# Memory attention's products in the other order, and which split the gathered rows follow

## The chip, the cores and the metric

The kernel runs on one core of one Trainium2 chip. The time is that of one launch on the device, in microseconds. Three runs of the kernel before took 4951.19, 4959.05 and 4960.37 us; their median is 4959.05 us. A further execution was profiled: it took 4954.55 us, and its trace spans 4952.8 us. All durations below are from that one trace.

The core has five instruction streams that run side by side and wait for one another by semaphores: TensorE (PE; its weight loads are shown apart, as PEld), VectorE (DVE), ScalarE (ACT), GpSimd (POOL), and SP, which here only issues transfers. POOL issues transfers too.

## The reference

One layer on 512 tokens of width 2048: a mixer (an mLSTM with 4 heads, a forgetting attention "fox" with 16 heads, two gated branches, an output product), then attention over a memory of 256 rows, then a layer of 16384 experts of which each token picks 128. Each of the three is followed by a residual and a norm. What is changed is the attention over the memory:

```python
def memory_cross_attention(x, mem, w_q, w_kv, w_o):
    q = (x @ w_q).reshape(B, S, X_HEADS, X_HD)          # 4 heads of 512
    kv = mem @ w_kv                                     # 256 x 4096
    k = kv[..., :D_MODEL].reshape(B, -1, X_HEADS, X_HD)
    v = kv[..., D_MODEL:].reshape(B, -1, X_HEADS, X_HD)
    s = jnp.einsum('bshd,bmhd->bhsm', q, k) * X_HD ** -0.5
    p = jax.nn.softmax(s, -1)
    o = jnp.einsum('bhsm,bmhd->bshd', p, v).reshape(B, S, D_MODEL)
    return o @ w_o
```

In the expert layer a token's output is the sum over its 128 experts of gelu(u.x) g v, where u and v are rows of two tables of 16384 x 2048.

## The kernel before

**Products.** A 2048-wide product runs in groups of 512 output columns. A group takes 8 loads; each load (`load_w`) brings 512 KB of weights into a buffer `raw` by a transfer from SP, ACT rounds it into a high part `whi` (L134), and DVE subtracts for the low part `wlo` (L137); with `work["share"]` at 8, POOL does every eighth subtraction instead (L136). PE then does three passes (high by high, high by low, low by high). `group_ws` holds the weights as the stationary operand: 24 matmuls for a load, as wide as there are tokens. `group_as` holds the activations: 6 matmuls of 512 columns for a load and block of 128 tokens. Plain f32 matmuls (scores, results) are not split.

**Two paths.** The first 128 tokens are path A, the other 384 path B. A has short work for a load (6 matmuls of 512), B long work (24 of 384, or 18 of 512). `weave(gen, other, rate)` takes `rate` steps of `other` for each step of `gen`, and one step at the end of a group of A. Small work between loads (scores, transposes) stands in a list `mids`, from which `ride` takes one step after each load's products. Loads go through `raw` buffers of two rings, 3 and 2 deep. Within this written order a planner that simulates the engines settles the order of each engine's instructions; SP, too, takes its transfers in order.

**Stages, with their places in the trace.** Memory keys and values (`memory`, 64 loads), woven with A's mLSTM, to 368 us. A's branch product (`branch_ml`, 64 loads), woven thinly with B's mLSTM ("heads"), to 514. A's fox (128 loads), woven likewise, to 822. A's merge, output product, norm, memory attention (`cross`, 32 loads for its queries), its output product (`residual` with `w_xo`, 32 loads), norm and expert query, woven likewise, to 1290. Then B: the rest of its mLSTM, branch, fox (1715 to 2320), merge, output product, `cross` (about 2630 to 2815), `residual` with `w_xo` (to 2963), query. Then the expert tables: from 3129 the choice of experts and products with U for the first `LOOK` = 72 of 128 blocks (`stage_a`), from 3636 the main loop, which multiplies by V and does the rest of U.

**Gathered rows.** For block A and for some tokens of B, rows of the tables come by indirect transfers that POOL issues (L846), and DVE multiplies or adds them (L874, L877, 2.3 us each). For block A these 258 steps are spread over 315 loads of path B, from B's mLSTM to its second residual. The instruction `after` ties each transfer and each use to `work["last"]`, the low-part split of the last load, whichever engine did it.

**Memory attention before.** `memory` writes keys transposed (`kmd`) and values (`vmd`) to DRAM: four groups of `group_ws` at 256 columns, four of `group_as` with two blocks. `cross` multiplies the tokens by `w_xq` head by head, then has f32 score matmuls (L719), a softmax (L723 to L726), transposes (L733) and f32 result matmuls (L741).

Of the kernel before, what the change touches and what calls it, by code (L numbers as in the profile page):

```python
# [46 lines left out]
def build(tc, I, out):  # L47
    nc = tc.nc
    with ExitStack() as ctx:
# [261 lines left out]
        vmd = dp.tile([X_H, 2, P, 512], F32, tag="vmd", name="vmd")  # L311
        mkd = dp.tile([ML_H, 2, P, P], F32, tag="mkd", name="mkd")
# [40 lines left out]
        def memory(mp):  # L353
# [8 lines left out]
            for g in range(4):  # L362
                def ev_mk(s, b, g=g, k=[]):
# [282 lines left out]
        def residual(R, pool, src, X, W, alloc, tmp, r, out):  # L646
# [3 lines left out]
            for g in range(4):  # L650
# [8 lines left out]
                yield from group_as(W[g], X, R.nb, ev)  # L659
# [39 lines left out]
        def cross(R, pool, X1, qt, kvt, pt, opair, O):  # L699
            n, nb = R.n, R.nb  # L700
            for h in range(X_H):
                q = []

                def ev_q(s, b, q=q):
                    q.append(qt())
                    nc.scalar.activation(q[s], b[:, :n], AF.Copy, scale=X_D ** -0.5)

                yield from R.group(I["w_xq"][h], X1, ev_q)
                kt2, v2 = ([kvt(), kvt()] for _ in range(2))
                for j in range(2):  # L710
                    nc.gpsimd.dma_start(kt2[j], kmd[h, j])
                    nc.gpsimd.dma_start(v2[j], vmd[h, j])
                pr, pT = [], []

                def scores(q=q, kt2=kt2, pr=pr):
                    for qb in range(nb):
                        bank = sm_bank()
                        for c in range(4):
                            nc.tensor.matmul(bank[:, :MEM], q[c][:, qb * P:(qb + 1) * P],  # L719
                                             kt2[c // 2][:, (c % 2) * MEM:(c % 2 + 1) * MEM], start=c == 0, stop=c == 3)  # L720
                        st = pool.tile([P, 4], F32, tag="xst", bufs=4, name=nm("xst"))
                        p = pool.tile([P, MEM], F32, tag="xp", bufs=nb, name=nm("xp"))
                        nc.vector.tensor_reduce(out=st[:, 0:1], in_=bank[:, :MEM], axis=AX.X, op=ALU.max, negate=True)  # L723
                        nc.scalar.activation(p, bank[:, :MEM], AF.Exp, bias=st[:, 0:1], accum_out=st[:, 1:2])
                        nc.vector.reciprocal(st[:, 2:3], st[:, 1:2])
                        nc.vector.tensor_scalar(p, p, st[:, 2:3], None, op0=ALU.mult)  # L726
                        pr.append(p)

                def turn_p(pr=pr, pT=pT):
                    for m in range(2):  # L730
                        bank = sm_bank()
                        for qb in range(nb):
                            nc.tensor.transpose(bank[:, qb * P:(qb + 1) * P], pr[qb][:, m * P:(m + 1) * P], ident)  # L733
                        pT.append(pt())
                        nc.scalar.copy(pT[m], bank[:, :n])

                def result(cs, h=h, v2=v2, pT=pT):
                    for c in cs:
                        bank = sm_bank()
                        for m in range(2):  # L740
                            nc.tensor.matmul(bank[:, :n], v2[m][:, c * P:(c + 1) * P], pT[m], start=m == 0, stop=m == 1)  # L741
                        a, b = opair(h)
# [4 lines left out]
                mid(scores, None, turn_p, lambda f=result: f((0, 1)), lambda f=result: f((2, 3)))  # L747
# [208 lines left out]
        with tc.tile_pool(name="sa", bufs=1, side="right", reuse_waits="tile") as sa:  # L956
            def aq(n=P):
                return sa.tile([P, P], F32, tag="q", bufs=11, name=nm("aq"))
# [26 lines left out]
            with tc.tile_pool(name="a1", bufs=1, side="right", reuse_waits="tile") as a1:  # L985
# [16 lines left out]
            def tail_a():  # L1002
                r, sts = [[None] * 4], []
                ra = {}
                with tc.tile_pool(name="a2", bufs=1, side="right", reuse_waits="tile") as a2:
# [9 lines left out]
                    yield from cross(A, sa, X1A, aq, at, aq, ac, OA)  # L1015
# [402 lines left out]
```

## Time and profile before

| | |
|---|---|
| median of three runs | 4959.05 us |
| profiled execution | 4954.55 us (span 4952.8 us) |
| PE busy | 4747.2 us, 96%, 28401 matmuls |
| DVE busy | 3713.1 us, 75% |
| ACT busy | 2123.3 us, 43% |
| POOL busy | 1416.2 us, 29% |
| transfers | 1420.99 MB, mean 287 GB/s |
| granted TensorE clock | 0.985 of full speed, mean |

The shares are of the span. A matmul is counted as busy from its start to its modelled end, and neighbours overlap: the time that a matmul takes of PE is read from the starts of matmuls in a row, not from its own duration. In a window row the columns are the length, then busy time and instruction count of each engine, the granted clock, the busy share of the transfer engines, and GB/s.

### The profile page before, as it was taken

The page shows a single profiled execution, that of the slowest core. Times are in us where ns is not written, and L with a number is a line of the kernel's source. Part 1 is how long each engine was busy: PE and PEld are TensorE (multiplying, and loading weights), DVE is VectorE, ACT ScalarE, POOL GpSimd, SP SyncE. Part 2 cuts the span into 40 slices and gives each one's busy share as a digit, 9 for nine tenths or more (in the row PEclk, how much of TensorE's full clock was granted, in tenths as well). Part 3 has the DMA queues.
Part 4 walks back from the last instruction along what each step waited for, and adds up shares of the span by engine and source line. Part 5 has one row for each costly group of instructions (what it writes and reads, how often), then busy time and mean ns, then how long its engine had stood idle before and what let it go on. Part 6 is the DMA issues. An engine that isn't in the chain of part 4 may idle for free. (4 is left out here: it accounts for less than half of the span.)

```text
span 4952.8 us, 74559 instructions
## 1 busy us (share of the span) xinstructions
PE 4747.2 (96%) x28401; PEld 4370.2 (88%) x28401; DVE 3713.1 (75%) x5355; ACT 2123.3 (43%) x3078; POOL 1416.2 (29%) x1039
## 2 busy tenths in 40 slices
PE   7999999999998999999899999999989999999997
PEld 6888778787788999999888988999989999999997
DVE  6676767766987776777775657799877888888785
ACT  5556666565532233333224324334444433333342
POOL 1122223221233534444442432322102222221220
PEclk9999999999999999999999999999999999999998
DMA  7788878866598998887895765577879999999883
GB/s 248 254 283 283 286 261 274 283 233 226 204 344 307 344 346 311 297 311 278 323 346 203 273 250 183 195 280 278 290 274 330 355 338 356 349 342 348 336 322 133
DMA packets 375416, 1420.99 MB, mean 287 GB/s; under 512 B 43340, under 2 KB 104396, under 8 KB 316016
## 3 DMA queue, kind: packets, MB, share of 16 engines
q1 hardware_dynamic: 263904, 827.14, 46.5%
q0 software_dynamic: 89408, 551.06, 29.9%
q10 hardware_dynamic: 21744, 38.02, 2.1%
q8 instruction: 222, 3.64, 0.3%
q14 instruction: 138, 1.13, 0.1%
HBM read 1343.32 MB, written 72.62 MB: 286 GB/s over the span
## 5 line engine op out<-in xcount | busy, mean ns | idle before, releaser
L134 ACT CAST whi<-raw 128x1024 fp32r<-128x1024 f32 x1472 | 1528.4, 1051 | 1887.7 <-PE mm L205 847.5
L137 DVE TENSOR_TENSOR wlo<-raw,whi 128x1024 fp32r<-128x1024 f32 x1352 | 1700.5, 1269 | 738.5 <-ACT whi L134 510.1
L846 POOL DMA_INDIRECT rows<-in_peer_v,eid x224 | 435.3, 1943 | 836.1 <-DVE wlo L137 457.8
L846 POOL DMA_INDIRECT rows<-in_peer_u,eid x224 | 363.2, 1622 | 939.0 <-DVE wlo L137 370.4
L877 DVE SCALAR_TENSOR_TENSOR xacc<-rows,dots,xacc 128x2048 f32<-128x2048 f32 x224 | 530.3, 2367 | 69.9 <-POOL wlo L136 38.5
L874 DVE SCALAR_TENSOR_TENSOR rows<-rows,xacc 128x2048 f32<-128x2048 f32 x224 | 518.9, 2318 | 71.0 <-DMA rows<-in_peer_u,eid 54.6
L205 PE MATMUL po<-hph,whi 128*128 128x288 f32 x2048 | 552.6, 297 | 18.4 <-ACT hph L134 14.4
L205 PE MATMUL sm<-Ch,whi 128*128 128x288 f32 x2048 | 561.0, 298 | 4.7 <-ACT whi L134 2.9
L205 PE MATMUL sm<-Cl,whi 128*128 128x288 f32 x2048 | 558.3, 297 | 0.0
L205 PE MATMUL po<-hpl,whi 128*128 128x288 f32 x2048 | 551.4, 297 | 0.1
L136 POOL TENSOR_TENSOR wlo<-raw,whi 128x1024 fp32r<-128x1024 f32 x120 | 300.7, 2506 | 734.7 <-ACT whi L134 499.8
L205 PE MATMUL mm<-xh,whi 128*128 128x384 f32 x1280 | 437.8, 344 | 16.0 <-ACT whi L134 11.1
L205 PE MATMUL mm<-xl,whi 128*128 128x384 f32 x1280 | 430.2, 338 | 0.0
L205 PEld LDWEIGHTS po<-hph,whi 128*128 128x128 f32 x2048 | 385.0, 189 | 21.5 <-ACT hph L134 15.5
L205 PEld LDWEIGHTS sm<-Ch,whi 128*128 128x128 f32 x2048 | 387.5, 189 | 6.9 <-ACT whi L134 3.1
L205 PEld LDWEIGHTS sm<-Cl,whi 128*128 128x128 f32 x2048 | 387.4, 189 | 0.8 <-issue 0.8
L205 PEld LDWEIGHTS po<-hpl,whi 128*128 128x128 f32 x2048 | 385.0, 189 | 1.2 <-issue 0.8
L205 PE MATMUL po<-hph,wlo 128*128 128x288 f32 x2048 | 329.9, 296 | 5.4 <-DVE wlo L137 5.3
L205 PE MATMUL sm<-Ch,wlo 128*128 128x288 f32 x2048 | 320.5, 297 | 4.1 <-DVE wlo L137 4.1
L205 PEld LDWEIGHTS po<-hph,wlo 128*128 128x128 f32 x2048 | 291.1, 188 | 8.0 <-DVE wlo L137 7.8
L205 PEld LDWEIGHTS sm<-Ch,wlo 128*128 128x128 f32 x2048 | 287.7, 189 | 5.6 <-DVE wlo L137 5.5
L205 PEld LDWEIGHTS mm<-xh,whi 128*128 128x128 f32 x1280 | 242.1, 189 | 24.9 <-ACT whi L134 12.8
(440 smaller groups left out, 8751.8 us busy)
## 6 DMA issues: line engine op xcount, KB each, us to landing
raw<-in_w_in SPq DMA_DIRECT2D x512, 512.0 KB
raw<-in_uT SPq DMA_DIRECT2D x256, 512.0 KB
raw<-in_vq SPq DMA_DIRECT2D x256, 512.0 KB
raw<-in_w_xkv SPq DMA_DIRECT2D x64, 512.0 KB
raw<-in_w_br_ml SPq DMA_DIRECT2D x64, 512.0 KB
raw<-in_w_br_fx SPq DMA_DIRECT2D x64, 512.0 KB
raw<-in_w_out SPq DMA_DIRECT2D x64, 512.0 KB
raw<-in_w_xq SPq DMA_DIRECT2D x64, 512.0 KB
```

The lines of the kernel that those rows point to most:

```text
L134: nc.scalar.copy(hi, src)
L136: return nc.gpsimd.tensor_sub(lo, src, hi.bitcast(F32))
L137: return nc.vector.tensor_sub(lo, src, hi.bitcast(F32))
L205: nc.tensor.matmul(o, w if stat else x, x if stat else w, start=k == first and x is xh and not part, stop=k == last and part == 1)
L846: i = nc.gpsimd.indirect_dma_start(out=rows, out_offset=None, in_=I[table], in_offset=bass.IndirectOffsetOnAxis(ap=ei[:, k:k + 1], axis=0))
L874: after(nc.vector.scalar_tensor_tensor(rows, rows, 1.0, xacc, op0=ALU.mult, op1=ALU.mult, accum_out=dots[:, k:k + 1]), last())
L877: after(nc.vector.scalar_tensor_tensor(xacc, rows, dots[:, k:k + 1], xacc, op0=ALU.mult, op1=ALU.add), last())
```

## The change

For each head the kernel now multiplies weights and memory first. M = w_q K^T / sqrt(512) for a head is 2048 x 256, and scores are x M; Z = V w_o for a head is 256 x 2048, and the output is the sum over heads of p Z. `memory_products` makes both from `kmd` and `vmd`, once for all tokens: 32 loads of w_q transposed (`group_ws` shape at 256 columns) and 32 loads of w_o (12 matmuls of 512 columns each), and writes them to DRAM as `md` and `zd` (8.4 MB each) in the form of weights. `cross` becomes two groups of `group_as` over `md` (two heads at once), each closed by the softmax, then transposes; `residual` runs over `zd` with 4 loads for a group instead of 8. Values are now made by `group_ws` as keys are.

The weave is rearranged: A's branch joins A's mLSTM beside `memory` (0.34 steps of it for a step of A); `memory_products` runs beside A's fox (0.38); B's mLSTM runs beside A's merge to query at 0.36 instead of 0.045, and no longer beside branch and fox.

`work["last"]` now keeps only DVE's own splits. The 258 gathered steps of block A are spread over 290 loads. `LOOK` is 76. The tile pool `q` has 10 buffers instead of 11.

```diff
-            hi, lo, work["last"] = load_pair(src, work["share"] and work["n"] % work["share"] == 0)
+            pool = work["share"] and work["n"] % work["share"] == 0
+            hi, lo, i = load_pair(src, pool)
+            if not pool:
+                work["last"] = i
...
-        def group_as(src, X, nt, evac):
+        def group_as(src, X, nt, evac, kts=8):
             banks = [mm_bank() if nt > 1 else ma_bank() for _ in range(nt)]
-            for kt in range(8):
+            for kt in range(kts):
                 wh, wl = load_w(src[kt])
                 todo = []
                 for t in range(nt):
@@ -235,9 +238,9 @@
                         xh, xl = X[2 * kt + kk]
                         c = slice(kk * 512, (kk + 1) * 512)
                         todo.append((banks[t], wh[:, c], wl[:, c], xh[:, tt], xl[:, tt], 2 * kt + kk, False))
-                products(todo, 0, 15)
+                products(todo, 0, 2 * kts - 1)
                 ride()
-                if kt < 7:
+                if kt < kts - 1:
...
+        md = dp.tile([2, 8, P, 2, 2, MEM], F32, tag="md", name="md")
+        zd = dp.tile([4, X_H, P, 1024], F32, tag="zd", name="zd")
...
-            for g in range(4):
-                def ev_mk(s, b, g=g, k=[]):
+            for g in range(8):
+                def ev(s, b, g=g, k=[]):
                     if s % 2 == 0:
                         k.append(mp.tile([P, 512], F32, tag="mo", bufs=1, name=nm("mo")))
                     nc.scalar.copy(k[-1][:, (s % 2) * MEM:(s % 2 + 1) * MEM], b[:, :MEM])
                     if s % 2:
-                        nc.gpsimd.dma_start(kmd[g, s // 2], k[-1])
-
-                yield from group_ws(I["w_xkv"][g], MT, MEM, ev_mk)
-            for g in range(4):
-                def ev_mv(t, b, g=g):
-                    v = mp.tile([P, 512], F32, tag="mo", bufs=1, name=nm("mo"))
-                    nc.vector.tensor_copy(v, b)
-                    nc.gpsimd.dma_start(vmd[g, t], v)
-
-                yield from group_as(I["w_xkv"][4 + g], MT, 2, ev_mv)
+                        nc.gpsimd.dma_start((kmd, vmd)[g // 4][g % 4, s // 2], k[-1])
+
+                yield from group_ws(I["w_xkv"][g], MT, MEM, ev)
...
+        def memory_products(zp):
+            def load(src):
+                t = [pair(zp, "kv", [P, 512], 8) for _ in range(2)]
+                for j in range(2):
+                    load_split(*t[j], src[j])
+                return t
+            def out():
+                return zp.tile([P, 1024], F32, tag="zo", bufs=2, name=nm("zo"))
+            K = load(kmd[0])
+            for h in range(X_H):
+                V = load(vmd[h])
+                for g in range(4):
+                    banks = [mm_bank() for _ in range(4)]
+                    for i in range(2):
+                        wh, wl = load_w(I["w_xqT"][g, 2 * h + i])
+                        todo = []
+                        for kk in range(2):
+                            kh, kl = (x[:, kk * MEM:(kk + 1) * MEM] for x in K[i])
+                            for s in range(4):
+                                c = slice(kk * 512 + s * P, kk * 512 + (s + 1) * P)
+                                todo.append((banks[s][:, :MEM], wh[:, c], wl[:, c], kh, kl, 2 * i + kk, True))
+                        products(todo, 0, 3)
+                        ride()
+                        if i == 0:
+                            yield
+                    o = out()
+                    for s in range(4):
+                        nc.scalar.activation(o[:, s * MEM:(s + 1) * MEM], banks[s][:, :MEM], AF.Copy, scale=X_D ** -0.5)
+                    for i in range(2):
+                        nc.gpsimd.dma_start(md[h // 2, 2 * g + i, :, :, h % 2],
+                                            o[:, i * 512:(i + 1) * 512].rearrange("p (k m) -> p k m", k=2))
+                    yield
+                if h < X_H - 1:
+                    K = load(kmd[h + 1])
+                for g in range(4):
+                    banks = [mm_bank() for _ in range(2)]
+                    for i in range(2):
+                        wh, wl = load_w(I["w_xo"][g, 2 * h + i])
+                        todo = []
+                        for m in range(2):
+                            for kk in range(2):
+                                vh, vl = (x[:, kk * MEM + m * P:kk * MEM + (m + 1) * P] for x in V[i])
+                                c = slice(kk * 512, (kk + 1) * 512)
+                                todo.append((banks[m], wh[:, c], wl[:, c], vh, vl, 2 * i + kk, False))
+                        products(todo, 0, 3)
+                        ride()
+                        if i == 0:
+                            yield
+                    o = out()
+                    for m in range(2):
+                        nc.vector.tensor_copy(o[:, m * 512:(m + 1) * 512], banks[m])
+                    nc.gpsimd.dma_start(zd[g, h], o)
+                    yield
...
-        def residual(R, pool, src, X, W, alloc, tmp, r, out):
+        def residual(R, pool, src, X, W, alloc, tmp, r, out, kts=8):
...
-                yield from group_as(W[g], X, R.nb, ev)
+                yield from group_as(W[g], X, R.nb, ev, kts)
...
-        def cross(R, pool, X1, qt, kvt, pt, opair, O):
+        def cross(R, pool, X1, opair, O):
+
             n, nb = R.n, R.nb
...
-                yield from R.group(I["w_xq"][h], X1, ev_q)
...
-                    nc.gpsimd.dma_start(kt2[j], kmd[h, j])
...
-                def scores(q=q, kt2=kt2, pr=pr):
...
+            for hp in range(2):
+                pr = [None] * nb
+
+                def ev(t, b, pr=pr):
+                    st = pool.tile([P, 8], F32, tag="xst", bufs=4, name=nm("xst"))
+                    p = pr[t] = pool.tile([P, 512], F32, tag="xp", bufs=nb, name=nm("xp"))
+                    nc.vector.tensor_reduce(out=st[:, 0:2], in_=b.rearrange("p (h m) -> p h m", h=2), axis=AX.X,
+                                            op=ALU.max, negate=True)
+                    for h in range(2):
+                        m = slice(h * MEM, (h + 1) * MEM)
+                        nc.scalar.activation(p[:, m], b[:, m], AF.Exp, bias=st[:, h:h + 1],
+                                             accum_out=st[:, 2 + h:3 + h])
+                    nc.vector.reciprocal(st[:, 4:6], st[:, 2:4])
+                    for h in range(2):
+                        m = slice(h * MEM, (h + 1) * MEM)
+                        nc.vector.tensor_scalar(p[:, m], p[:, m], st[:, 4 + h:5 + h], None, op0=ALU.mult)
+
+                def turn_p(ms, pr=pr):
+                    for m in ms:
                         bank = sm_bank()
...
-                def turn_p(pr=pr, pT=pT):
...
-                def result(cs, h=h, v2=v2, pT=pT):
...
+                        for t in range(nb):
+                            nc.tensor.transpose(bank[:, t * P:(t + 1) * P], pr[t][:, m * P:(m + 1) * P], ident)
+                        a, b = opair()
                         nc.scalar.copy(a, bank[:, :n])
                         nc.vector.tensor_sub(b, bank[:, :n], a.bitcast(F32))
                         O.append((a, b))
-                mid(scores, None, turn_p, lambda f=result: f((0, 1)), lambda f=result: f((2, 3)))
+                yield from group_as([md[hp, kt].rearrange("p k h m -> p (k h m)") for kt in range(8)], X1, nb, ev)
+                mid(lambda f=turn_p: f((0, 1)), lambda f=turn_p: f((2, 3)))
...
-                return sa.tile([P, P], F32, tag="q", bufs=11, name=nm("aq"))
+                return sa.tile([P, P], F32, tag="q", bufs=10, name=nm("aq"))
...
-                    weave(first, mem, 52 / 77)
+                    weave(chain(first, branch_ml(A, HA, aq)), mem, 0.34)
...
-                    yield from cross(A, sa, X1A, aq, at, aq, ac, OA)
-                    yield from residual(A, sa, lambda t, g: x1d[t, :, g], OA, I["w_xo"], alloc, at, r, sts)
+                    yield from cross(A, a2, X1A, ac, OA)
+                    yield from residual(A, sa, lambda t, g: x1d[t, :, g], OA, zd, alloc, at, r, sts, 4)
...
+            with tc.tile_pool(name="mz", bufs=1, reuse_waits="tile") as zp, \
+                    tc.tile_pool(name="a3", bufs=1, side="right", reuse_waits="tile") as a3:
+                mix = memory_products(zp)
+                weave(fox(A, a3, at, hold_y), mix, 0.38)
+                run(mix)
+                settle()
...
-            with tc.tile_pool(name="a3", bufs=1, side="right", reuse_waits="tile") as a3:
-                weave(chain(branch_ml(A, HA, aq), fox(A, a3, at, hold_y)), heads, 0.045)
-                weave(iter([2]), heads, 0)
-                settle()
-            weave(chain(merge(A, YA, GA, ac, at), tail_a()), heads, 0.045)
+            weave(chain(merge(A, YA, GA, ac, at), tail_a()), heads, 0.36)
...
-        work.update(jobs=gathered(0, 0, P, 0, lambda: work["last"], 2), rate=258 / 315)
+        work.update(jobs=gathered(0, 0, P, 0, lambda: work["last"], 2), rate=258 / 290)
...
-            run(cross(B, xp, X1, lambda: a_tile(B.n), kvt, lambda: tmp(),
-                      lambda h: cpair() if h == 3 else pair(apool, "A", [P, B.n], 32), O))
-            run(residual(B, xp, lambda t, g: x1d[t, :, g], O, I["w_xo"], lambda i: a_tile() if i < 8 else kvt(),
-                         tmp, r, sts))
+            run(cross(B, xp, X1, lambda: pair(apool, "A", [P, B.n], 32), O))
+            run(residual(B, xp, lambda t, g: x1d[t, :, g], O, zd, lambda i: a_tile(), tmp, r, sts, 4))
...
-        LOOK = 72
+        LOOK = 76
...
+    r["w_xqT"] = _groups(np.ascontiguousarray(a["w_xq"][0].T))
```

More of the change, by code (lines that the diff above doesn't have):

```diff
@@ L696, in norm @@
             work.update(hold=False, quiet=4, normed=i_last)
-        def cross(R, pool, X1, qt, kvt, pt, opair, O):
+        def cross(R, pool, X1, opair, O):
             n, nb = R.n, R.nb
[L701 to L706, printed above, removed]
-                yield from R.group(I["w_xq"][h], X1, ev_q)
-                kt2, v2 = ([kvt(), kvt()] for _ in range(2))
-                for j in range(2):
-                    nc.gpsimd.dma_start(kt2[j], kmd[h, j])
-                    nc.gpsimd.dma_start(v2[j], vmd[h, j])
-                pr, pT = [], []
-                def scores(q=q, kt2=kt2, pr=pr):
-                    for qb in range(nb):
-                        bank = sm_bank()
[L718 to L727, printed above, removed]
-                def turn_p(pr=pr, pT=pT):
[L730 to L735, printed above, removed]
-                def result(cs, h=h, v2=v2, pT=pT):
[L738 to L742, printed above, removed]
@@ L1101, in tmp @@
                 return xp.tile([P, n], F32, tag="t", bufs=6, name=nm("t"))
-            def kvt():
-                return xp.tile([P, 512], F32, tag="k", bufs=4, name=nm("k"))
             def a_tile(n=512):
@@ L1387, in layout @@
     r["ln_bT"] = _cols(a["ln_b"][0])
-    for n, k in (("w_br_ml", "w_branch_ml"), ("w_br_fx", "w_branch_fox"), ("w_out", "w_out"), ("w_xq", "w_xq"),
+    for n, k in (("w_br_ml", "w_branch_ml"), ("w_br_fx", "w_branch_fox"), ("w_out", "w_out"),
                  ("w_xkv", "w_xkv"), ("w_xo", "w_xo"), ("peer_wq", "peer_wq")):
         r[n] = _groups(a[k][0])
+    r["w_xqT"] = _groups(np.ascontiguousarray(a["w_xq"][0].T))
     r["x"] = x
```

## The prediction

> **What bounds the kernel now.** I read the page first, then the table of windows with one window for each stage, then the timeline for the time that one matmul takes of TensorE, then the waits. The page's line of engines, and its line of transfers:
>
> ```profile
> PE 4747.2 (96%) x28401; PEld 4370.2 (88%) x28401; DVE 3713.1 (75%) x5355; ACT 2123.3 (43%) x3078; POOL 1416.2 (29%) x1039
> ...
> DMA packets 375416, 1420.99 MB, mean 287 GB/s; under 512 B 43340, under 2 KB 104396, under 8 KB 316016
> ```
>
> TensorE is busy in 96% of the span, so the sum must be one of TensorE's time, and every other engine matters only where it makes TensorE wait. The windows, stage by stage (memory; A's branch; A's fox; A's merge to query; B's fox; B's memory attention; its output product; the main loop):
>
> ```profile
> core 0: us, PE busy (x) PEld busy (x) DVE busy (x) ACT busy (x) POOL busy (x), PEclk, DMA share, GB/s
> 64.00:368.00 304.00, 296.99 (x1660) 257.02 (x1661) 210.47 (x292) 180.80 (x216) 58.54 (x43) 0.99 0.78 270
> 368.00:514.00 146.00, 139.63 (x659) 117.14 (x658) 101.40 (x114) 92.19 (x115) 34.04 (x31) 1.00 0.81 279
> 514.00:822.00 308.00, 301.20 (x1400) 243.62 (x1399) 208.55 (x309) 199.39 (x285) 77.30 (x77) 1.00 0.81 276
> 822.00:1290.00 468.00, 446.74 (x2048) 360.34 (x2046) 325.95 (x528) 271.32 (x393) 107.68 (x110) 0.99 0.71 251
> 1715.00:2320.00 605.00, 604.71 (x3335) 565.53 (x3335) 447.05 (x552) 213.96 (x328) 267.74 (x173) 1.00 0.85 312
> 2630.00:2815.00 185.00, 176.59 (x962) 164.68 (x962) 119.35 (x133) 73.65 (x121) 73.53 (x49) 0.97 0.67 249
> 2815.00:2963.00 148.00, 148.00 (x666) 122.77 (x665) 87.77 (x80) 41.48 (x52) 55.06 (x35) 1.00 0.71 265
> 3636.00:4830.00 1194.00, 1158.07 (x8580) 1145.30 (x8579) 965.74 (x1143) 460.85 (x638) 272.39 (x162) 0.98 0.90 336
> ```
>
> TensorE idles 7.0, 6.4, 6.8 and 21.3 us in the four A stages (41.5 of 1226 us), 8.4 and 0.0 in B's two, 36 in the main loop (3.0%). B's fox shows TensorE without a gap at 312 GB/s of transfers, and the main loop nearly so at 336.
>
> **The change part by part: TensorE.** What a matmul takes is the distance between starts. The timeline merges runs of the same matmul; a run's length less one matmul's own duration, over one fewer than its count, is that distance. First the runs, then the groups with each form's mean duration and count:
>
> ```profile
> 157.43 1.12 PE L205 MATMUL mm<-mth,wlo 128*128 128x256 f32 x8
> 2680.22 1.55 PE L205 MATMUL mm<-Ch,wlo 128*128 128x384 f32 x8
> 2711.62 1.24 PE L719 MATMUL sm<-k,ra 128*128 128x256 f32 x5
> 2724.98 2.74 PE L741 MATMUL sm<-t,k 128*128 128x384 f32 x8
> 2851.51 1.53 PE L205 MATMUL mm<-wlo,Ah 128*128 128x512 f32 x6
> ```
>
> ```profile
> L205 PE MATMUL mm<-Ch,wlo 128*128 128x384 f32 x512 | 103.3, 336 | 0.5 <-DVE wlo L137 0.5
> ...
> L205 PE MATMUL mm<-mth,wlo 128*128 128x256 f32 x256 | 38.0, 285 | 0.5 <-DVE wlo L137 0.5
> ...
> L205 PE MATMUL mm<-wlo,Ah 128*128 128x512 f32 x144 | 37.4, 389 | 0.0
> ...
> L741 PE MATMUL sm<-t,k 128*128 128x384 f32 x64 | 22.6, 485 | 0.0
> ...
> L719 PE MATMUL sm<-k,ra 128*128 128x256 f32 x96 | 22.0, 379 | 0.0
> ...
> L741 PE MATMUL sm<-aq,at 128*128 128x128 f32 x64 | 8.6, 278 | 1.0 <-DVE Cl L744 0.8 <-ACT aq L735 0.2
> ...
> L719 PE MATMUL sm<-at,aq 128*128 128x256 f32 x32 | 7.9, 379 | 0.0
> ```
>
> So a product matmul takes 0.120 us at 256 columns ((1.12-0.285)/7), 0.173 at 384, 0.228 at 512. A plain f32 matmul takes 0.215 at 256 columns and 0.322 at 384, and stands in the trace twice: 96 rows of L719 for B's 4 x 3 x 4 scores. These are the costliest columns of the attention.
>
> Before, in us: keys 768 x 0.120 = 92.2; values 384 x 0.228 = 87.6; A's queries and A's output product, 192 matmuls of 512 each, 43.8 + 43.8; B's queries 768 x 0.173 = 132.9; B's output product 576 x 0.228 = 131.3; scores 96 x 0.215 + 32 x 0.215 = 27.5; results 64 x 0.322 = 20.6 and, for A at a third of the columns, 64 x 0.107 = 6.9; A's 16 query transposes 1.7. Sum 588.3.
>
> After: keys and values 1536 x 0.120 = 184.3; M 768 x 0.120 = 92.2; Z 384 x 0.228 = 87.6; A's two halved products 2 x 96 x 0.228 = 43.8; B's 2 x 288 x 0.228 = 131.3; the transposes of p stay as many (8 and 24). Sum 539.2. TensorE saves **49 us**. About 174 us leave B's last stages and 60 leave A's tail, while 185 come into the A phase: the sum is a difference of large terms, and it holds only if what comes in is covered as well as what goes.
>
> The Trainium skill, page "TensorE: Matmul & The Clock Gate", section "Back-to-back issue gap", gives N/2.4 + 2.5 ns for a warm matmul; by it the product matmuls would come to 498.8 us before and 500.2 after, and the saving would be some 55 us. The rows lie 10 to 12 ns above that for each matmul, and the rows decide.
>
> **A's stages.** Loads stay as many (192 in these parts), so ACT's and DVE's splits do too; what moves is which loads lie beside which. By the yields in the code, 38 steps of B's heads go with A's merge to query now and 70 after, and the 33 beside branch and fox go. At 0.228 and 0.173 a B load takes 4.1 us. The first stage becomes 304 + 146 - 9 x 4.1 + 5 = 418 us, fox 308 - 23 x 4.1 + 180 = 393, the tail 468 - 60 + 31 x 4.1 = 535. At fox's present idle share (2.2%) these 1346 us would idle 30 us, at the tail's (4.5%) 61, against 41.5 now: -11 to +20. I take 0: the tail gets more cover for its norms, fox gets more traffic.
>
> Fox with the products is the new place. Its bytes: 276 GB/s x 308 us = 85.0 MB now, less 23 loads of 0.524 (12.1), plus 64 loads (33.6), the writes of `md` and `zd` (16.8) and the reads of `kmd` and `vmd` (4.2): 127.5 MB in 393 us, 324 GB/s. That lies between the two rates above at which TensorE hardly waits, but with loads that A uses up three times as fast. ACT there rises from 199 us by 41 loads and 64 evacuations, DVE from 209 by 41 loads and 32 evacuations:
>
> ```profile
> L137 DVE TENSOR_TENSOR wlo<-raw,whi 128x1024 fp32r<-128x1024 f32 x1352 | 1700.5, 1269 | 738.5 <-ACT whi L134 510.1 <-PE mm L205 183.3 <-PE ma L205 19.3
> L134 ACT CAST whi<-raw 128x1024 fp32r<-128x1024 f32 x1472 | 1528.4, 1051 | 1887.7 <-PE mm L205 847.5 <-PE po L205 270.7 <-PE sm L205 205.5
> ```
>
> ```profile
> L723 DVE TENSOR_REDUCE xst<-sm x16: 400/416/427, 1068.9 to 2846.7; 128x1 f32<-128x256 f32 x16
> L724 ACT ACTIVATE xp<-sm,xst x16: 465/474/485, 1069.6 to 2847.2; 128x256 f32<-128x256 f32 x16
> ```
>
> With 1.05 and 1.27 us a load, an evacuation at 0.47 (ACT, 256 columns) and 0.83 (DVE, 512 columns, twice L723), that is 273 and 288 us of 393: neither binds. The waits that bear on it, ACT's in A's fox and then TensorE's over the span:
>
> ```profile
> ACT whi L134 <- DMA raw<-in_w_in: 45.9, 29, 3.0
> ```
>
> ```profile
> PE sm L682 <- DVE ra L675: 13.0, 2, 6.5
> ...
> PE mm L205 <- DVE Al L142: 7.0, 6, 3.1
> PE mm L205 <- ACT Ah L141: 6.6, 8, 2.7
> ```
>
> Idle at the main loop's 3.0% would be 12 us instead of 6.8: +5. Keys and values come through `load_split` on SP's queue, 16 loads: the next head's V waits until TensorE has done the last Z product, and the weight transfers of two or three steps stand behind it on SP; behind the `md` issues on POOL, which wait for ACT's evacuations, stand POOL's splits. The nearest row is B's merge, where 16 such loads (Al, Ah) cost 13.6 us; with A's steps between I take 5, between 0 and 13.6. Together **+10**, from 0 up to the rival's price below.
>
> **B's stages.** `cross` closes two groups with a softmax. A bank is free after a reduction (0.83 by the estimate above), a table load and two exponentials:
>
> ```profile
> L724 ACT ACT_TABLE_LOAD x1 | 1.3, 1283 | 0.0
> ```
>
> 0.83 + 1.28 + 2 x 0.47 is 3.1 us. Of five banks two are free, and the next group's first two blocks, 8 matmuls, cover 1.8. The transposes then wait for all three blocks' chains, 4.1 us of products ahead of them. I take 2 us for each of two places, **+4**; the ends are 6 each, and -2, since of the window's 8.4 us now 6.5 belong to the norm (L682's longest wait). The residual's groups of 4 loads keep three banks of five and one evacuation each, as now.
>
> **Gathered rows.** 258/290 instead of 258/315 is 0.89 a load instead of 0.82. Waits of DVE from 1290 to 2963, and one use:
>
> ```profile
> DVE xacc L877 <- POOL wlo L136: 38.5, 11, 5.5
> ```
>
> ```profile
> L877 DVE SCALAR_TENSOR_TENSOR xacc<-rows,dots,xacc 128x2048 f32<-128x2048 f32 x224 | 530.3, 2367 | 69.9 <-POOL wlo L136 38.5 <-DMA rows<-in_peer_v,eid 29.3
> ```
>
> In B's fox (128 loads) DVE goes from 3.49 us a load to 3.49 + 0.07 x 2.37 = 3.66 of 4.73: still 77%, with TensorE at 604.71 of 605. **+3**, between 0 and 46 (the 20 steps that the shorter stages no longer carry, all uncovered). The tie to DVE's own splits takes away up to 38.5 us of DVE's waiting in stages where DVE does not bind: **-2**, between 0 and -38.5.
>
> **76 keys.** Four blocks of U, some 25 us of TensorE, move ahead of the main loop, and its gathered steps come 2% denser. A 3.0% idle share on 25 us is 0.8; 2% of 36 us is 0.7 the other way: **0**, within 5 each way.
>
> Sum: -49 + 10 + 4 + 3 - 2 = -34. The profiled execution took 4954.55 us, 4.5 less than the median of three; the prediction is **4920 us**.
>
> **The rivals.** *The weave gains more.* A's idle falls to fox's 2.2%, and neither the products stage nor B's softmax nor the denser gathers cost anything: -49 - 11 - 2, 4893 us. For it: the tail idles most now and gets twice the cover. Against: its gaps are chains of norm and softmax, which stay.
>
> *The transfers bind the products stage (slower).* Fox with the products needs 324 GB/s; at the 276 which this stage shows now it takes 462 us, 69 more: 4979 us. At the mean rate of 287 it takes 444, 51 more: 4961. It decides below 292 GB/s (437 us, 44 more, which with the other +5 uses up the 49). For it: ACT already waits 45.9 us for weights there, with five `raw` buffers in all, and the new writes share the same transfer engines. Against: 276 is what TensorE asked for, not a ceiling that the trace shows.
>
> *Stationary loads count.* The product matmuls rise from 2880 to 3456, each with its own load:
>
> ```profile
> L205 PEld LDWEIGHTS mm<-mth,wlo 128*128 128x128 f32 x256 | 34.2, 194 | 1.2 <-DVE wlo L137 1.0
> ```
>
> If each added its 194 ns, 576 more are +112 us: 5018 us. The same form's matmuls start every 0.120 us, so the load is hidden. The same page of the Trainium skill ("What overlaps and what doesn't") says that loads overlap matmuls in flight only when their row groups differ; all here use all 128 rows, and the trace does not agree.
>
> *The denser gathers uncover DVE*: +46 in place of +3, 4963 us. *The tie does nothing*: the sum moves by 2.
>
> **How the numbers follow.** 0.2% is 9.9 us, about what a measurement of this kernel can tell from no change. The forecast, 4905 to 4940, has 0.50; the weave 0.18; the transfers 0.23 (0.10 within 0.2%, 0.13 slower); stationary loads 0.02; gathers 0.05 (0.02 and 0.03); a gain between these 0.02. Faster 0.70, same 0.12, slower 0.18. The range goes from just beyond the weave's time to the transfers' full price, 4888 to 4979.
>
> **What would show it.** Right: L719 and L741 f32 forms gone; some 3456 products in these parts at 0.12 and 0.23 us; A's fox and products near 400 us at 315 GB/s or more with TensorE idle under 20 us; B's `cross` and second residual together near 160 us instead of 333; no DVE use waiting for POOL's split. Wrong: TensorE waiting for `whi` in fox with ACT waiting for `raw`, or gaps over 5 us at B's softmax.

## The result, and the profile after

The changed kernel takes 4907.32 us (median of four runs, 4899.57 to 4913.27) beside 4956.37 us for the kernel before: a ratio of 0.9901, interval 0.9881 to 0.992. Measured again on another chip it took 4898.83 us, ratio 0.9884 (0.9868 to 0.99). It is 49 to 56 us faster; 4920 had been predicted. The first time lies at the lower end of the forecast's 4905 to 4940, the second below it, nearer to the 4893 us of the weave rival.

The profiled execution took 4913.27 us, the longest of its four. The page's lines of engines and of transfers:

```profile
PE 4713.5 (96%) x28705; PEld 4353.5 (89%) x28705; DVE 3736.2 (76%) x5363; ACT 2127.7 (43%) x3106; POOL 1351.3 (28%) x1055
...
DMA packets 380027, 1433.60 MB, mean 292 GB/s; under 512 B 43853, under 2 KB 104909, under 8 KB 320625
```

TensorE is still busy in 96% of a shorter span. There are 304 more matmuls, but narrow ones. The windows by stage: A with memory and branch; A's fox with the products; A's merge to query with B's mLSTM; B's fox; B's `cross`; its residual; the main loop.

```profile
64.00:490.00 426.00, 408.87 (x2480) 361.11 (x2481) 292.62 (x365) 260.20 (x325) 88.22 (x69) 0.98 0.83 280
490.00:883.00 393.00, 374.04 (x2027) 313.66 (x2026) 257.79 (x321) 250.68 (x386) 113.71 (x118) 0.99 0.89 310
883.00:1415.00 532.00, 521.90 (x2438) 434.73 (x2438) 360.17 (x652) 287.31 (x391) 118.40 (x114) 0.99 0.67 220
...
1840.00:2445.00 605.00, 603.06 (x3323) 563.35 (x3323) 468.53 (x554) 212.67 (x326) 249.84 (x183) 1.00 0.89 329
...
2757.00:2854.00 97.00, 87.38 (x408) 70.96 (x407) 69.72 (x88) 46.05 (x78) 34.14 (x32) 0.95 0.67 246
2854.00:2924.00 70.00, 68.74 (x304) 55.26 (x303) 66.64 (x72) 23.45 (x35) 25.29 (x19) 1.00 0.89 320
...
3636.00:4800.00 1164.00, 1129.26 (x8348) 1116.77 (x8349) 942.02 (x1091) 444.82 (x595) 255.77 (x161) 0.98 0.91 339
```

Idle time of TensorE is the length less the busy time: 17.1, 19.0 and 10.1 us in the A stages, 1.9 in B's fox, 10.9 in B's two, 34.7 in the main loop. Where the time went is read from the issues of certain weight loads, which mark the same places in both traces:

| from, to | before, us | after, us | change | products alone |
|---|---|---|---|---|
| start, B's merge | 2320 | 2445 | +125 | +125 |
| B's merge and output product | 310 | 312 | +2 | 0 |
| B's `cross` and residual | 333 | 167 | -166 | -174 |
| B's query and experts' choice | 166 | 163 | -3 | 0 |
| first U block, end | 1824 | 1824 | 0 | 0 |

The last column is the prediction's own sum split by path: in A's phase keys and values +4.5, M 92.2, Z 87.6, less 103.1 of A's old attention, plus 43.8 of its new one. So 125 us of work came in ahead of B and cost 125; 174 left B, of which 166 were gained.

The forms that replace the f32 ones, from the groups of instructions kept apart by shape (one pass of three each):

```profile
L208 PE MATMUL mm<-mth,wlo 128*128 128x256 f32 x512 | 74.5, 283 | 0.2 <-DVE wlo L137 0.2
...
L208 PE MATMUL mm<-kvh,wlo 128*128 128x256 f32 x256 | 38.2, 283 | 0.0
```

A group of eight of the new form, from the timeline, gives the distance between starts: (1.12 - 0.283)/7 = 0.120 us, as taken.

```profile
517.48 1.12 PE L208 MATMUL mm<-kvh,wlo 128*128 128x256 f32 x8
```

Waits in A's fox with the products (total, times, longest):

```profile
ACT whi L134 <- DMA raw<-in_w_in: 44.5, 33, 4.3
...
ACT whi L134 <- DMA raw<-in_w_xo: 23.3, 18, 3.7
...
ACT whi L134 <- DMA raw<-in_w_xqT: 7.3, 7, 2.0
...
PE mm L208 <- ACT whi L134: 5.6, 6, 1.6
...
PE ma L208 <- ACT whi L134: 4.0, 5, 2.3
```

```profile
SPq L148 <- DVE wlo L137: 184.9, 126, 4.6
SPq L148 <- POOL wlo L136: 42.3, 19, 3.7
...
SPq L140 <- PE mm L208: 7.2, 9, 1.4
```

ACT waits 75 us for weights here. SP, which issues them, stands 227 of the 393 us before a split by DVE or POOL, that is, before a buffer that is still in use. This pair of waits became the question of the experiments. SP's wait alone is no sign of trouble: in B's fox of the kernel before, where TensorE idled 0.3 us, SP stood so for 447 of 605 us.

```profile
SPq L148 <- DVE wlo L137: 356.7, 88, 10.7
SPq L148 <- POOL wlo L136: 90.2, 16, 7.3
```

### The profile page after: what moved, and what is told of

Same layout as the page of the kernel before. It is cut to its first block, busy times and chain, and to the rows that moved or that the text cites. A ratio compares the mean times of both kernels' runs of the same rounds, so it can differ in the third digit from the quotient of the medians.

```text
span 4911.5 us, 75235 instructions
## 1 busy us (share of the span) xinstructions
PE 4713.5 (96%) x28705; PEld 4353.5 (89%) x28705; DVE 3736.2 (76%) x5363; ACT 2127.7 (43%) x3106; POOL 1351.3 (28%) x1055
## 5 line engine op out<-in xcount | busy, mean ns | idle before, releaser
L885 POOL DMA_INDIRECT rows<-in_peer_v,eid x224 | 379.6, 1695 | 815.0 <-DVE xacc L916 431.4
L885 POOL DMA_INDIRECT rows<-in_peer_u,eid x224 | 322.2, 1438 | 1009.4 <-DVE rows L913 357.8
L916 DVE SCALAR_TENSOR_TENSOR xacc<-rows,dots,xacc 128x2048 f32<-128x2048 f32 x224 | 542.0, 2420 | 40.2 <-DMA rows<-in_peer_v,eid 38.9
L208 PE MATMUL po<-hph,wlo 128*128 128x288 f32 x2048 | 340.9, 297 | 1.4 <-DVE wlo L137 1.3
```

Of the source, the lines that this page charges most:

```text
L208: nc.tensor.matmul(o, w if stat else x, x if stat else w, start=k == first and x is xh and not part, stop=k == last and part == 1)
L885: i = nc.gpsimd.indirect_dma_start(out=rows, out_offset=None, in_=I[table], in_offset=bass.IndirectOffsetOnAxis(ap=ei[:, k:k + 1], axis=0))
L916: after(nc.vector.scalar_tensor_tensor(xacc, rows, dots[:, k:k + 1], xacc, op0=ALU.mult, op1=ALU.add), last())
```

## The experiments

**The half with M alone.** Scores go through M; values, results and `w_xo` stay as they were, with the weave and the spread of the gathers cut to fit.

```diff
...
-                    nc.gpsimd.dma_start(zd[g, h], o)
...
+                        for m in range(2):
+                            nc.tensor.matmul(bank[:, :n], vs[d][m][:, c * P:(c + 1) * P], pTs[d][m],
+                                             start=m == 0, stop=m == 1)
...
-                    yield from residual(A, sa, lambda t, g: x1d[t, :, g], OA, zd, alloc, at, r, sts, 4)
+                    yield from residual(A, sa, lambda t, g: x1d[t, :, g], OA, I["w_xo"], alloc, at, r, sts)
...
-                weave(fox(A, a3, at, hold_y), mix, 0.38)
+                weave(fox(A, a3, at, hold_y), mix, 0.15)
...
-        work.update(jobs=gathered(0, 0, P, 0, lambda: work["last"], 2), rate=258 / 290)
+        work.update(jobs=gathered(0, 0, P, 0, lambda: work["last"], 2), rate=258 / 295)
```

> Half of the change: scores through M, but values, results and the output product as before (V from memory with two blocks, f32 result matmuls, w_xo in full), with the changed kernel's weave (32 product loads beside A's fox at 0.15; gathers at 258/295). Theory (the gain is TensorE's sum): M's half saves 205.9 - 179.8 = 26 us of TensorE, so about 4930 us, 26 below the kernel before and 23 above the changed one. Rival (the gain comes from the rearranged weave, which covers A's tail better): the weave is the same, so nearly the whole 49 us stay, about 4910 us.

Measured: 4959.54 us, ratio 1.0008 (0.9996 to 1.002). Its matmuls are 26 us shorter by count and distance, and nothing of that was gained. Its windows of A's fox and of B's merge, B's merge in the kernel before, and TensorE's longest waits in the M half's merge:

```profile
484.00:801.00 317.00, 291.59 (x1643) 249.15 (x1641) 200.62 (x258) 209.29 (x334) 97.98 (x100) 0.97 0.87 301
2402.00:2588.00 186.00, 167.24 (x896) 159.84 (x895) 133.19 (x117) 53.07 (x76) 81.03 (x76) 0.95 0.86 317
```

```profile
2322.00:2500.00 178.00, 163.11 (x885) 155.05 (x885) 128.22 (x116) 52.35 (x74) 80.79 (x74) 0.97 0.85 320
```

```profile
PE mm L208 <- ACT Ah L141: 11.6, 5, 4.8
PE mm L208 <- DVE Al L142: 5.1, 3, 3.5
```

Fox idles 25.4 us where 6.8 were idle before, and B's merge takes 186 us instead of 178 (four of these eight are idle time, four busy time, at a granted clock of 0.95 instead of 0.97). These two take the 26. So a gain of TensorE in this kernel isn't safe until the stage that receives the work is looked at.

**A thin weave in the tail.** B's mLSTM goes with A's merge to query as thinly as before.

```diff
-            weave(chain(merge(A, YA, GA, ac, at), tail_a()), heads, 0.36)
+            weave(chain(merge(A, YA, GA, ac, at), tail_a()), heads, 0.045)
...
-        work.update(jobs=gathered(0, 0, P, 0, lambda: work["last"], 2), rate=258 / 290)
+        work.update(jobs=gathered(0, 0, P, 0, lambda: work["last"], 2), rate=258 / 325)
```

> The changed kernel with B's heads at 0.045 instead of 0.36 beside A's merge to query, as before the change (and gathers at 258/325, since some 35 B loads more are left for their stage). Theory (TensorE's sum): the tail idles about as it did before, 21 us instead of 10, and little else moves: 4907 + 10, at most 25 more. Rival (the weave makes the gain): 30 to 49 us are lost, 4937 to 4956 us.

Measured: 4918.81 us, ratio 0.9914 (0.989 to 0.9939), 11 us above the changed kernel's first median and 20 above its second.

```profile
884.00:1281.00 397.00, 367.38 (x1682) 299.86 (x1681) 278.39 (x468) 227.33 (x322) 88.30 (x91) 0.98 0.73 242
```

The tail idles 29.6 us instead of 10.1, where 21 had been expected. With the heads that are then left it takes 765 us, and 741 as changed. The weave is worth 11 to 20 us by the medians, though this run's interval overlaps that of the first measurement; most of the gain stays without it.

**Products written twice.** `md` and `zd` are written to a second place too, 16.8 MB that nobody reads.

```diff
...
+                        for dst in (md, md2):
+                            nc.gpsimd.dma_start(dst[h // 2, 2 * g + i, :, :, h % 2],
...
                     nc.gpsimd.dma_start(zd[g, h], o)
+                    nc.gpsimd.dma_start(zd2[g, h], o)
```

> The changed kernel, which writes each piece of md and zd a second time to a copy that nobody reads: 16.8 MB more in A's fox stage (121.8 MB in 393 us now, 310 GB/s). Theory (the transfers are covered there): at the 340 GB/s which other stages of this kernel show it would take 408 us, so 0 to 15 us more, 4907 to 4922 us. Rival (the transfers bind at what the stage shows): 138.6 MB at 310 GB/s are 447 us, 54 more, 4961 us.

Measured: 4940.04 us, ratio 0.9963 (0.9951 to 0.9975), 33 us above the changed kernel's first median and 41 above its second, between the two expectations. Most of it lies in A's fox (422 us instead of 393):

```profile
486.00:908.00 422.00, 380.23 (x2020) 312.32 (x2019) 253.19 (x319) 248.89 (x385) 144.96 (x165) 0.98 0.90 324
```

```profile
PE ma L208 <- ACT whi L134: 21.7, 19, 2.0
...
PE ma L208 <- POOL wlo L136: 4.5, 4, 1.3
...
PE mm L208 <- ACT whi L134: 3.3, 5, 0.9
```

The transfers moved more per second than in the changed kernel (324 against 310 GB/s), so 310 was no ceiling; and still TensorE idled 41.8 us instead of 19.0. Its waits for `whi` rise from 9.6 to 25.0 us, those for POOL's splits only from 3.2 to 4.5, which speaks against the queue on POOL, which issues the writes, as what holds it up. With more traffic the weights are ready later: matched in order, ACT begins to round a load 8.2 us (median) after its transfer was issued, and 7.3 us in the changed kernel. ACT's waits for landings are no longer than there (69 us against 75), so how much of this is the transfer and how much ACT's own delay isn't shown.

**A quarter of the scores, in the kernel before.**

```diff
-                        for c in range(4):
+                        for c in range(1):
                             nc.tensor.matmul(bank[:, :MEM], q[c][:, qb * P:(qb + 1) * P],
-                                             kt2[c // 2][:, (c % 2) * MEM:(c % 2 + 1) * MEM], start=c == 0, stop=c == 3)
+                                             kt2[c // 2][:, (c % 2) * MEM:(c % 2 + 1) * MEM], start=True, stop=True)
```

> The kernel before with only the first of the four score matmuls of each block and head (three quarters of the scores are left out, so its result is not the reference's). 96 of the 128 rows of L719 go, at 0.215 us each. Theory (f32 matmuls count with every row that the trace shows): 20.6 us less than before, about 4936 us. Rival (they stand beside waits, or one of the two rows is not real time): 0 to 10 us less.

Measured: 4934.89 us, ratio 0.9953 (0.9937 to 0.997), 22 us less, where 96 rows x 0.215 is 20.6. The rows of path B that are left, from the groups of instructions:

```profile
L719 PE MATMUL sm<-k,ra 128*128 128x256 f32 x24 | 5.8, 379 | 0.0
```

Each f32 matmul's two rows are both TensorE time; the scores' and results' part of the sum stands.

**A third ring in A's fox.** Only there, the weights get three more raw buffers (eight instead of five) and one more each for the high and the low part.

```diff
-            with tc.tile_pool(name="mz", bufs=1, reuse_waits="tile") as zp, \
+            with tc.tile_pool(name="mz", bufs=1, reuse_waits="tile") as zp, ExitStack() as rs, \
                     tc.tile_pool(name="a3", bufs=1, side="right", reuse_waits="tile") as a3:
+                three = list(rings)
+                rings.append(weights(rs, "w3", 3, 1, 1))
                 mix = memory_products(zp)
                 weave(fox(A, a3, at, hold_y), mix, 0.38)
                 run(mix)
                 settle()
+                rings[:] = three
```

> The changed kernel with a third ring of weight buffers (3 raw, 1 high, 1 low) in A's fox with the products alone: eight raw buffers instead of five. In that stage a weight transfer takes 5.5 us (median) from its issue to its landing, and ACT waits 75 us for weights. Theory (the stage is paced by how many loads are under way): TensorE's 19 us of idle time there fall to some 5 to 9, and the kernel takes 4890 to 4897 us, 10 to 17 below the changed one. Rival (the transfer engines are at their limit, at 0.89 busy and 310 GB/s): no more than 3 us either way. Rival (TensorE's sum and nothing else): no change.

Measured: 4888.71 us, ratio 0.9869 (0.9854 to 0.9884): the best time of this study.

```profile
486.00:856.00 370.00, 357.12 (x2002) 309.57 (x2001) 260.26 (x318) 251.42 (x383) 114.54 (x118) 0.99 0.90 331
```

```profile
ACT whi L134 <- DMA raw<-in_w_in: 8.5, 6, 2.4
...
PE mm L208 <- ACT whi L134: 7.2, 1, 7.2
...
PE ma L208 <- ACT whi L134: 0.6, 2, 0.4
```

```profile
SPq L148 <- DVE wlo L137: 192.0, 126, 8.1
SPq L148 <- POOL wlo L136: 38.1, 16, 5.1
```

The same bytes pass at 331 instead of 310 GB/s, and the stage is 19 to 23 us shorter. TensorE idles 12.9 us there instead of 19.0, more than the 5 to 9 expected. ACT's largest wait for weights falls from 44.5 to 8.5 us, its waits for their landing in all from 75 to 10. SP stands before a used buffer as long as it did, 230 us: what changed is that the weights have landed when ACT wants them. The transfers weren't at their limit: too few were under way. That the raw buffers did it, and not the extra high and low part, is likely, since ACT's waits for TensorE to give back a high part rose (47 to 72 us); a run with raw buffers alone is missing.

**M's first loads multiplied again.** The first load of each group for heads 0 and 1: 192 more matmuls of 256 columns, 23 us of TensorE, and no more loads.

```diff
+                        if i == 0 and h < 2:
+                            products(todo, 0, 1)
                         products(todo, 0, 3)
```

> The changed kernel, in which the first of the two loads of each product M of heads 0 and 1 is multiplied twice (the second time over the first, so the result stays): 8 loads x 24 matmuls x 0.120 = 23 us more of TensorE in A's fox stage, and not one load more. Theory (TensorE's sum counts in full): 23 us more, 4930 us. Rival (the stage is paced by its loads, about 2.0 us each, and TensorE has room there): 5 to 12 us more, 4912 to 4919 us.

Measured: 4921.56 us, ratio 0.9939 (0.9924 to 0.9954): 14 us above the changed kernel's first median, 23 above its second. The window of A's fox is 15 to 19 us longer (408 us against 393 and 389); from the start of the trace to A's merge it is 9 to 14.

```profile
484.00:892.00 408.00, 392.26 (x2221) 336.59 (x2220) 255.75 (x321) 251.72 (x386) 114.70 (x118) 0.99 0.86 299
```

By this window and by the whole kernel more than half of the 23 us come out as time, so the loads don't set the pace all through the stage.

To compare these runs, count x distance was summed over every matmul that starts in A's fox, and the sum taken from the length of the window. What is left is time lost between matmuls, the slack within long busy stretches too:

| kernel | window, us | matmuls, us | lost, us |
|---|---|---|---|
| before | 308 | 293 | 15 |
| M half | 317 | 277 | 40 |
| M half, third ring | 291 | 273 | 17 |
| changed | 393 | 358 | 35 |
| changed, second measurement | 389 | 357 | 32 |
| third ring | 370 | 353 | 17 |
| M's first loads again | 408 | 382 | 26 |
| written twice | 422 | 357 | 65 |

**The M half with the third ring.** The two edits above together.

> The half change (M alone) with the third ring of buffers in A's fox. The half gained nothing where TensorE's sum gave 26 us. Theory (its loads beside A's fox came closest together, 1.8 us of TensorE for each, and the stage was paced by them): the ring brings back 12 to 20 us, 4940 to 4948 us. Rival (what it lost lies in B's merge, memory attention and elsewhere): 0 to 8 us.

Measured: 4927.31 us, ratio 0.9944 (0.9928 to 0.9961), 32 us below the M half, more than expected. Fox and B's merge:

```profile
484.00:775.00 291.00, 277.56 (x1614) 243.37 (x1614) 200.98 (x257) 209.06 (x329) 94.91 (x96) 0.98 0.92 331
2374.00:2550.00 176.00, 159.95 (x889) 152.87 (x888) 135.28 (x117) 52.76 (x76) 83.83 (x75) 0.99 0.90 332
```

26 us come from fox. Ten come from B's merge (176 against 186), where the ring no longer exists: TensorE idles 16.0 us there instead of 18.8, and the other seven are shorter busy time for the same products, at a granted clock of 0.99 instead of 0.95. Why the clock differs isn't shown, so these seven aren't put down to the ring. With loads no longer late, the kernel is 28 us below the kernel before on the same chip (4955.06), about the 26 of the M half's sum. The half with Z wasn't run alone: between this run and the whole change with the ring and 72 blocks on the same chip (4893.58, below) lie 34 us, where the sum gives 23.

**The tie alone, in the kernel before.**

```diff
-            hi, lo, work["last"] = load_pair(src, work["share"] and work["n"] % work["share"] == 0)
+            pool = work["share"] and work["n"] % work["share"] == 0
+            hi, lo, i = load_pair(src, pool)
+            if not pool:
+                work["last"] = i
```

> The kernel before with the one edit that work["last"] keeps DVE's own splits. Theory: DVE no longer waits 38.5 + 14.3 us for POOL's splits, but it does not bind there: 0 to 5 us less than before, about 4954 us. Rival (DVE's waits were TensorE's): 20 us less or more.

Measured: 4961.91 us, ratio 1.0014 (1.0005 to 1.0023), 7 us slower. DVE's waits for POOL's split are gone and nothing was gained. TensorE's first wait in B's merge:

```profile
PE mm L208 <- DVE Al L142: 14.2, 5, 7.1
```

It stood at 7.0 us before. Of that stage's ten more us it explains seven.

**The changed kernel without the tie.** The reverse edit.

> The changed kernel with work["last"] as before: the last low-part split of either engine. In the kernel before, the tie to DVE's splits alone made it 7 us slower, all of it in B's merge, where the wait for Al's splits doubled. Theory (an accident of order in the merge): the changed kernel's merge takes 177 us with the tie, as the kernel before does without it, so it has not paid here, and without the tie nothing changes: within 5 us. Rival (the tie costs wherever it stands): 7 us less. Second rival (it helps, as DVE's waits for POOL suggest): 5 us more.

Measured: 4911.24 us (4904.59 to 4921.94), ratio 0.9917 (0.99 to 0.9933), beside 4898.83 us with the tie on the same chip. DVE waits for POOL's split again:

```profile
DVE xacc L913 <- POOL wlo L136: 17.7, 7, 3.3
```

But all stages up to the main loop agree between the two traces within 3 us, the main loop is 7 us longer, and the profiled executions differ by 2.7 us. Three of the six runs lie at 4905 to 4906 us, inside the changed kernel's first measurement (4899.57 to 4913.27), and the median is 4 us above that one's. Where the 12 us between the medians lie isn't shown.

**72 blocks of U ahead instead of 76.**

```diff
-        LOOK = 76
+        LOOK = 72
```

> The changed kernel with 72 keys of U ahead, as before. Theory: 25 us of TensorE go from the stage ahead into the main loop, both equally filled: within 5 us of the changed kernel. Rival (76 relieves the main loop): 8 us more or above.

Measured: 4896.4 us, ratio 0.9879 (0.9864 to 0.9894). From the first U block to the end the trace has 1818 us; the changed kernel had 1824 and 1817. No difference.

**The changed kernel again**, and **the third ring with 72 blocks**, on one chip:

> The changed kernel itself, beside the three others on one chip, to compare them with. 0.990 of the kernel before again, about 4907 us.

> The changed kernel with the third ring in A's fox and with 72 keys of U ahead. Theory (76 keys change nothing): the same as with the ring alone, 4889 within 5 us. Rival (72 is better, as the run with 72 alone came out 11 us below the changed kernel): 4878 us.

Measured: 4898.83 us, ratio 0.9884 (0.9868 to 0.99), and 4893.58 us, ratio 0.9874 (0.9855 to 0.9893). The ring's stage is again 23 us shorter (796 us from the memory stage to A's merge against 819), but the whole is only 5 us shorter, and these intervals overlap. A's tail and B's merge took 4 us more each, the experts 7. The ring's 23 us in its stage are shown twice; of the whole it is worth 5 to 19.

## Why the prediction was right, and where its terms were off

**TensorE, -49.** Right, and it is the gain. Over the whole trace count x distance falls from 4647 to 4597 us, by 49 before rounding. The 576 more stationary loads cost nothing: the new form's matmuls start every 0.120 us as the old ones did, and the 125 us that the sum moves ahead of B cost 125; the Trainium skill's rule in "TensorE: Matmul & The Clock Gate", "What overlaps and what doesn't", taken by itself, would have them stand in the open, and the trace doesn't agree.

**A's stages, 0.** Lengths of 418, 393 (403 with fox's +10) and 535 us were forecast; 426, 393 and 532 came. TensorE's idle time in A is 46.2 us, where 41.5 + 10 had been forecast, but it lies elsewhere: the tail gave back 11 us, the memory stage took 4 more, fox 12 more. Two misses of opposite sign cancel here; that the sum comes so near is luck. That the tail's gaps would stay because they are chains was wrong: twice the cover halved them, as the thin weave shows.

**Fox with the products, +10.** Its idle time grew by 12 us, its lost time by 17 to 20. The term was 5 for late weights and 5 for the K and V loads; the first was too small, the second too large (SP's waits for TensorE there sum to 7.2 us, 1.4 at most, and TensorE has no wait for a K or V split among its five longest). The bytes were 121.9 MB at 310 GB/s, not 127.5 at 324.

**The transfer rival** had the right place and the wrong mechanism. It set a rate, and decided below 292 GB/s. The stage ran at 310, with more bytes at 324, with more buffers at 331. The prediction's sign for it, TensorE waiting for `whi` with ACT waiting for `raw`, was there (9.6 and 75 us), and the rate stayed under the 315 GB/s that it named for being right. What delayed weights was the number of buffers: five, each of 512 KB, a transfer 5.5 us from issue to landing (median of the transfers whose landing the trace shows), after it two splits of 1.05 and 1.22 us. That is 7.8 us for a buffer's turn, by estimate 1.6 us a load at best. Loads came every 2.1 us on average and closer together in stretches, so five buffers turned in some 10 us: the rest of the turn went in waiting for ACT and DVE. The Trainium skill's page "Perfetto Trace Analysis", section "Optimization Strategy", says that a gap which repeats on the engine that should be saturated can mean too few buffers; the ring's lost time of 17 us instead of 32 to 35 agrees.

**B's softmaxes, +4.** The two windows idle 10.9 us instead of 8.4, +2.5; by count x distance the time lost there goes from 14 to 20 us, about +6. 6.5 us are one wait of the norm, as before, and no wait for a softmax is long:

```profile
PE sm L738 <- DVE ra L731: 6.5, 1, 6.5
...
PE mm L208 <- ACT xp L768: 0.3, 1, 0.3
```

**Gathers, +3.** TensorE idles 1.9 us in B's fox, DVE is busy 77% there as forecast: at most 2.

**The tie, -2.** The waits it removes were worth nothing, as argued, but what it does to the order in B's merge cost 7 us alone. Between +7 there and -4 to -12 in the changed kernel its price isn't settled.

**76 keys, 0.** Right.

The added terms, +15 in the forecast, came to +8 between the two profiled executions, to 0 between the first medians and to -7 between the second. The forecast was right because its large term was; the small ones were partly wrong in both directions.

## What to carry to other kernels

Where two products by weights stand in a row, multiply the weights first when one side is short; but count what the work costs in the stage that receives it, since the M half saved 26 us of TensorE and gained nothing there. When the engine that uses weights waits for them to land, a rate below what other stages reach isn't a ceiling, and more buffers can help with the bytes as they are. That the issuing queue stands before a used buffer is no sign by itself, since it stood so just as long with eight buffers. Small edits of order can move several us at an unrelated place, so a part measured alone doesn't add up with the rest.

## What the runs showed that was not expected

- With five weight buffers, loads in A's fox came every 2.0 to 2.1 us in the kernel before, the M half and the changed kernel alike, though TensorE had between 1.7 and 1.9 us of work for each. With eight, the same bytes go at 331 GB/s instead of 310 and the lost time halves. Whether the raw buffers or the extra high and low part did it wasn't separated.
- 16.8 MB of writes that nobody reads cost 33 to 41 us, most of it in a stage at 310 GB/s: 2.0 to 2.4 us for each MB, though the mean rate rose.
- The tie made the kernel before 7 us slower and, by the medians, the changed one 4 to 12 us faster.
